# Two more ordinary block pairs, reuse of split weights at a half change, and two weight buffers instead of three

## The chip, the cores and the metric

The kernel runs on one core of one Trainium2 chip. The metric is the device time of the program in microseconds (us), the median of three runs; lower is better. TensorE (PE) multiplies matrices out of SBUF into PSUM, VectorE (DVE), ScalarE (ACT) and GpSimd (POOL) do the elementwise work, and SyncE (SP) holds the queue from which all transfers of this kernel are issued.

## The reference, cut to what matters

Three network blocks follow each other on one activation of 1024 tokens by 1024 features in float32. Two of them end in a feed-forward part, and these are what the change touches:

```python
# end of the first block: w_up is 1024 x 4096, w_down 4096 x 1024
up = jnp.square(jax.nn.relu(jnp.einsum('bsd,df->bsf', h2, w_up[l])))
x = x + jnp.einsum('bsf,fd->bsd', up, w_down[l])
...
# end of the third (last) block: w_up is 1024 x 5632, w_down 2816 x 1024
u = h @ w_up                                    # 5632 = 2 x 2816 columns
u = lax.conv_general_dilated(u, ...) + conv_b   # three taps along the tokens
gate, val = jnp.split(u, 2, axis=-1)
y = (jax.nn.gelu(gate, approximate=True) * val) @ w_down
x = x + rms_norm_3(y, ffn_post_norm[l])
```

## The kernel before, in words

Activations lie with features on the 128 partitions, in 8 blocks of features, and the 1024 tokens are cut into two halves of 512. Each float32 operand of a product is split in two parts, `hi` (a rounded copy, made on ACT) and `lo` (the rest, a subtraction on DVE or POOL); a product is then three matmuls, hi by hi, hi by lo and lo by hi (`mm3`, lines 179, 180, 181). `Env.split` (lines 143 and 145) makes the two parts.

`Env.chunk` loads one weight block (line 152, a 512 KB transfer on SP's queue for a full block) into a buffer `raw` and splits it into `whi` and `wlo`. Each of the three names has two buffers in the pool `wp`. Inside `e.third()` a further pool `wx` gives a third `whi` and `wlo`; `e.turn` counts the chunks, and every third one goes to `wx`.

**Ordinary units.** `Env.dense` multiplies one weight block with one half of the tokens: 8 blocks of features by three matmuls, 24 matmuls of 512 columns. In the last block, a feed-forward pair is a gate block `f` and its value block `22 + f`. The first `n0 = 4` pairs are done in ordinary units (line 1923): a loop over the two halves, in each over the four pairs, in each over the two blocks, so 16 units and 384 matmuls; the weight of each unit is loaded and split anew, so each block's weight twice. A unit is followed by the convolution (`conv`, lines 1897 to 1902, and `conv_rest`, lines 1907 and 1908), then by the GELU (line 1914) or the product and its store to DRAM (`put_up`, lines 1917 and 1918). In the first half, three steps of a generator (`join` for the second half of the tokens: residual, norm and split, lines 1454 to 1456, 250, 254, 263 and 143/145) are taken after each unit; what is left of it is run at the change of halves. In the second half each unit takes one step of `right_forms` (the sums and differences of activation blocks that the next part needs, lines 762 to 773), and the last two units one step of `left_forms` (the same for weights, lines 789 to 814).

**Strassen units.** The other 18 pairs go through `strassen`: each pair, both halves of the tokens, in seven products of four block steps, 84 matmuls instead of the 96 that a pair takes in ordinary units. Its weight forms use the buffers of `wp` as work space. In its last unit the loading of the down product's first activations (`FfnDown.load`, line 896 and a split) is interleaved.

**Down product.** `FfnDown.run` multiplies groups of up to six stored blocks by their weights: one chunk for each output block, which serves both halves (36 matmuls in a group of six), except in the last group, where the halves follow each other and each chunk serves one product of 15 matmuls. In the last block this runs inside `with e.third()`, opened after the pool `str` of the Strassen stage (its `c` tiles are what `put_up` stores from) is closed. While the second half of the last group is multiplied, the first half's residual and norm run (`end`).

The first block's feed-forward has the same stages with `n0 = 6` single blocks per half (line 690, 12 units), 13 Strassen units, and its down product runs with the two buffers of `wp` alone.

**What sets the order.** The program is written in the order above, but a planner at build time orders each engine's instructions by a simulated timeline (`schedule_with_timeline_sim=True`): an instruction whose inputs the simulation has ready can move ahead of ones written earlier that wait. On the chip each engine then runs its own list strictly in order, and SP its queue of transfers.

Of the kernel before, what the change touches and what calls it, by code (L numbers as in the profile page):

```python
# [46 lines left out]
class Ring:  # L47


    def __init__(self, views):  # L50
        self.views, self.i = views, 0

    def next(self):
        v = self.views[self.i % len(self.views)]
        self.i += 1
        return v
# [294 lines left out]
def block1(e, next_gain):  # L351


    nc, tc, io = e.nc, e.tc, e.io
# [4 lines left out]
    def load_x(h, ks=range(NK)):  # L359
        xs = []  # L360
        for k in ks:
            if k % 2 == 0:
                x = e.slot("x0")
            nc.sync.dma_start(x[:, k % 2], io["xT"][k][:, half(h)])
            xs.append(x[:, k % 2])
        return xs
# [3 lines left out]
    xs, hs, rc = [load_x(0, range(4))], [], []  # L370
# [292 lines left out]
    hs = [[], []]  # L663
    for f in range(0, NK, 4):
        ws = e.chunk(io["w1_out"][f : f + 4, :, 6:].rearrange("f p k o -> p f (k o)"), (4, 256), pool_lo=True)
        for j in range(4):
            w = [t[:, j].rearrange("p (k o) -> p k o", k=2) for t in ws]
# [12 lines left out]
    with ExitStack() as c2:  # L680
        tmp = c2.enter_context(tc.tile_pool(name="str", bufs=8))

        def act(f, h, src, dst):

            nc.scalar.activation(dst, src, AF.Relu)
            nc.scalar.activation(dst, dst, AF.Square)
            nc.sync.dma_start(upd[f, :, h], dst)

        n0 = 6
        fm, w = {}, {}  # L690
        weight = lambda u, i: io["w1_up"][n0 + 2 * u + i]
        forms, left = iter(()), iter(())
        units = [(f, h) for h in range(2) for f in range(n0)]
        wc = e.chunk(io["w1_up"][0])
        for i, (f, h) in enumerate(units):
            if i == n0:
                for _ in steps:
                    pass
                xs = [[a[:, j] for a in acc] for j in range(2)]
                acc.clear()  # L700
                forms, left = right_forms(e, xs, hs, fm), left_forms(e, weight, 0, w, tmp)
            p = e.dense(wc, hs[h])
            if i + 1 < len(units):
                wc = e.chunk(io["w1_up"][units[i + 1][0]])
            act(f, h, p, tmp.tile([P, HALF], F32, tag="c", name="c"))
            next(steps, None)
            next(forms, None)
            if h and f >= n0 - 2:
                next(left, None)
        hs = p = None  # L710
        for _ in left:
            next(forms, None)
        for _ in forms:
            pass

        def post(u, i, h, p):
            act(n0 + 2 * u + i, h, p, tmp.tile([P, HALF], F32, tag="c", name="c"))

        down = FfnDown(e, (6, 6, 5, 5, 5, 5), upd, io["w1_down"])
        strassen(e, tmp, fm, (32 - n0) // 2, weight, post, w, down.load(0))  # L720
        fm.clear()

# [22 lines left out]
def right_forms(e, xs, hs, fm):  # L745

    nc = e.nc
    fm.update(B11=hs[0][:4], B21=hs[0][4:], B22=hs[1][4:], T1=[], T2=[], T3=[], T4=[])

    def put(name, t):
        y = e.slot("act", dt=F32R)
        e.split(y[:, 0], y[:, 1], t)
        fm[name].append(y)

    for k in range(4):  # L760
        b11, b12, b22 = xs[0][k], xs[1][k], xs[1][k + 4]
        nc.vector.tensor_tensor(b11, b12, b11, op=ALU.subtract)
        nc.vector.tensor_tensor(b12, b22, b12, op=ALU.subtract)
        nc.vector.tensor_tensor(b22, b22, b11, op=ALU.subtract)
        put("T2", b22)
        put("T1", b11)
        yield
    for k in range(4):
        put("T3", xs[1][k])
        yield  # L770
    for k in range(4):
        b21, b22 = xs[0][k + 4], xs[1][k + 4]
        nc.vector.tensor_tensor(b21, b21, b22, op=ALU.subtract)
        put("T4", b21)
        yield
    for x in xs:
        x.clear()
# [44 lines left out]
def strassen(e, tmp, fm, n, weight, post, w, then):  # L822

    nc = e.nc  # L830

    def product(p, w, a, b, start, last):
        y, x = w.pop(a), fm.pop(b) if last else fm[b]
        for k in range(4):
            e.mm3(p, (y[:, 0, k], y[:, 1, k]), (x[k][:, 0], x[k][:, 1]), start and k == 0, k == 3, True)

    def first(w, last):
        ps = [e.pd() for _ in range(3)]
        product(ps[0], w, "A11", "B11", True, last)
        nc.scalar.activation(ps[1], ps[0], AF.Copy)  # L840
        return ps

    ps = first(w, n == 1)
    for u in range(n):
        last = u == n - 1
        nxt = {}
        pre = iter(()) if last else left_forms(e, weight, u + 1, nxt)

        def step():
            next(pre, None)  # L850
            if last:
                for _ in range(2):
                    next(then, None)

        product(ps[2], w, "S1", "T1", True, last)
        c22 = e.tsq()
        nc.scalar.activation(c22, ps[2], AF.Copy)
        step()
        product(ps[1], w, "S2", "T2", False, last)
        c12 = e.tnt()  # L860
        nc.scalar.activation(c12, ps[1], AF.Copy)
        step()
        product(ps[0], w, "A12", "B21", False, last)
        post(u, 0, 0, ps[0])
        step()
        product(ps[1], w, "S3", "T3", False, last)
        nc.vector.tensor_tensor(c22, ps[1], c22, op=ALU.add)  # L867
        step()
        follow = None if last else first(nxt, u + 2 == n)
        product(ps[1], w, "A22", "T4", False, last)  # L870
        post(u, 1, 0, ps[1])
        post(u, 1, 1, c22)
        step()
        product(ps[2], w, "S4", "B22", False, last)
        nc.vector.tensor_tensor(c12, ps[2], c12, op=ALU.add)
        post(u, 0, 1, c12)
        step()
        w, ps = nxt, follow
    for _ in then:
        pass  # L880


class FfnDown:
# [623 lines left out]
def block3(e, acc, hs, rest, out):  # L1507
    nc, tc, io = e.nc, e.tc, e.io
# [38 lines left out]
    with ExitStack() as c2:  # L1547
# [213 lines left out]
        units = [(i, h) for i in range(4) for h in range(2)]  # L1761
# [8 lines left out]
        order = (0, 4, 1, 5, 2, 6, 3, 7)  # L1770
# [17 lines left out]
    hs = [[], []]  # L1788
# [95 lines left out]
    hs = hn  # L1884
# [25 lines left out]
    def gelu(f, h, p, c):  # L1910
        conv(f, p, h, c)
        if h:
            conv_rest(f, c)
        nc.scalar.activation(c, c, AF.Gelu_apprx_tanh)
# [5 lines left out]
    with ExitStack() as c2:  # L1920
        tmp = c2.enter_context(tc.tile_pool(name="str", bufs=8))
        new = lambda: tmp.tile([P, HALF], F32, tag="c", name="c")
        n0 = 4
        fm, w = {}, {}
        weight = lambda u, i: io["w3_up"][n0 + u + 22 * i]
        forms, left = iter(()), iter(())
        units = [(b, h) for h in range(2) for f in range(n0) for b in (f, 22 + f)]
        wc = e.chunk(io["w3_up"][0])
        for i, (b, h) in enumerate(units):
            if i == 2 * n0:  # L1930
                for _ in steps:
                    pass
                forms, left = right_forms(e, xn, hs, fm), left_forms(e, weight, 0, w, tmp)
            p = e.dense(wc, hs[h])
            if i + 1 < len(units):
                wc = e.chunk(io["w3_up"][units[i + 1][0]])
            c = new()
            if b < 22:
                gelu(b, h, p, c)
                cg = c  # L1940
            else:
                conv(b, p, h, c)
                if h:
                    conv_rest(b, c)
                put_up(b - 22, h, cg, c)
            for _ in range(3):
                next(steps, None)
            next(forms, None)
            if h and i >= len(units) - 2:
                next(left, None)  # L1950
        hs = hn = p = c = cg = None
        for _ in left:
            next(forms, None)
        for _ in forms:
            pass

        cs = {}

        def post(u, i, h, p):

            f = n0 + u
            c = new()
            if i == 0:
                gelu(f, h, p, c)
            else:
                conv(22 + f, p, h, c)
                if h:
                    conv_rest(22 + f, c)
            cs[i, h] = c
            if i != h:  # L1970
                put_up(f, h, cs.pop((0, h)), cs.pop((1, h)))

        down = FfnDown(e, (6, 6, 5, 5), upd, io["w3_down"])
        strassen(e, tmp, fm, 22 - n0, weight, post, w, down.load(0))
        fm.clear()

# [12 lines left out]
        yield  # L1989
        yield from add_x(e, ms, xs, g_fpost, r, [o[:, half(h)] for o in out], True)  # L1990

    with e.third():
        for _ in down.run(add, end):
            pass


def prep3(a):
# [71 lines left out]
```

## Time and profile before

| | |
|---|---|
| runs | 3394.65, 3396.74, 3396.5 us; median 3396.5 us |
| the profiled execution | 3399.09 us, its span 3397.3 us |
| mean granted TensorE clock | 0.97 of full speed |
| PE busy | 3174.9 us, 93% of the span |
| DVE busy | 2119.8 us, 62% |
| ACT busy | 1504.1 us, 44% |
| POOL busy | 698.0 us, 21% |

The span is the time from the first to the last instruction of the one execution that was profiled. Busy shares are means over stages with different limits. The first block's ordinary units begin at about 599 us of the span, its down product runs from about 930 us; the last block's ordinary units begin at 2667.7 us, its Strassen units end at 3123.3 us and its down product follows to 3377.9 us.

### The profile page before, as it was taken

To read this page: it belongs to the slowest core of one execution; us is meant where nothing else is said; L and a number is where in the kernel's file an instruction comes from. 1 tells how busy PE (TensorE), PEld (TensorE's weight loads), DVE (VectorE), ACT (ScalarE), POOL (GpSimd) and SP (SyncE) were. 2 spreads that over 40 slices of the span, in tenths; PEclk is the share of its full clock that TensorE was granted. 3 is DMA by queue.
4 is the path that set the end of the run, shared out by engine and by line. 5 is a ranking of instruction groups with operands and counts; after the bars stand their busy time and mean duration, and the time that the engine had idled before them with its cause. 6 is when DMAs were issued, how large, how long until landed. Compare 5 with 4: busy or idle time off the path is not lost.

```text
span 3397.3 us, 43416 instructions
## 1 busy us (share of the span) xinstructions
PE 3174.9 (93%) x16044; PEld 2645.4 (78%) x16044; DVE 2119.8 (62%) x3795; ACT 1504.1 (44%) x2710; POOL 698.0 (21%) x451
## 2 busy tenths in 40 slices
PE   7999999999999998889999899989999989998997
PEld 6789877788888877667677777778887768886886
DVE  7666566654435366965776567666636687886336
ACT  4454453454532123433644565654434444454312
POOL 3000024000000004521444444435333200000001
PEclk9999999999999999899999899999999999998999
DMA  4112134433444234355644122225422432223333
GB/s 130 41 57 61 54 112 155 143 109 109 143 130 131 75 96 136 97 141 178 199 158 127 59 66 66 84 79 180 131 69 99 149 99 83 85 79 100 121 114 102
DMA packets 157572, 369.17 MB, mean 109 GB/s; under 512 B 20912, under 2 KB 29488, under 8 KB 157360
## 3 DMA queue, kind: packets, MB, share of 16 engines
q1 hardware_dynamic: 157360, 366.40, 33.8%
q8 instruction: 126, 2.06, 0.3%
q14 instruction: 86, 0.70, 0.1%
HBM read 286.64 MB, written 72.88 MB: 106 GB/s over the span
## 4 chain that ended last, share of the span: by engine, by line
PE 35%; DVE 9%; ACT 3%; issue 2%; DMA 1%; POOL 1%; SPq 0%; DVEq 0%; ACTq 0%; POOLq 0%
PE ps_d L179 10%; PE ps_d L180 10%; PE ps_d L181 10%; ACT whi L143 1%; DVE act L145 1%; DVE acc L1454 1%; POOL wlo L145 1%; PE ps_s L1737 1%; DVE hE L1723 0%; DVE wlo L145 0%; DVE hSA L1738 0%; DVE acc L1455 0%; DVE pr L1650 0%; DVE ssum L254 0%; PE ps_o L1320 0%
## 5 line engine op out<-in xcount | busy, mean ns | idle before, releaser
L143 ACT ACTIVATE whi<-raw 128x1024 fp32r<-128x1024 f32 (+2 forms) x328 | 317.3, 968 | 711.6 <-PE ps_d L180 601.9
L179 PE MATMUL ps_d<-act,whi 128*128 128x512 f32 x1280 | 512.8, 401 | 24.5 <-DVE acc L316 8.1
L181 PE MATMUL ps_d<-act,wlo 128*128 128x512 f32 x1280 | 508.4, 398 | 20.4 <-DVE wlo L145 19.5
L180 PE MATMUL ps_d<-act,whi 128*128 128x512 f32 x1280 | 508.9, 398 | 6.8 <-DVE act L145 6.7
L145 POOL TENSOR_TENSOR wlo<-raw,whi 128x1024 fp32r<-128x1024 f32 (+1 forms) x134 | 326.0, 2436 | 446.4 <-ACT whi L143 427.9
L179 PE MATMUL ps_d<-up,whi 128*128 128x512 f32 x864 | 337.5, 391 | 11.0 <-ACT whi L143 11.0
L179 PE MATMUL ps_d<-act,ws 128*128 128x512 f32 x868 | 335.0, 390 | 3.8 <-DVE sq L867 1.9
L180 PE MATMUL ps_d<-act,ws 128*128 128x512 f32 x868 | 338.4, 390 | 0.0
L180 PE MATMUL ps_d<-up,whi 128*128 128x512 f32 x864 | 337.2, 390 | 0.0
L181 PE MATMUL ps_d<-up,wlo 128*128 128x512 f32 x864 | 336.8, 390 | 0.0
L181 PE MATMUL ps_d<-act,ws 128*128 128x512 f32 x868 | 336.2, 390 | 0.0
L219 POOL TENSOR_TENSOR rr<-rv,mhalf 128x4 f32<-128x4 f32 (+1 forms) x43 | 45.6, 1060 | 1363.4 <-DVE rv L209 1177.2
L179 PEld LDWEIGHTS ps_d<-act,whi 128*128 128x128 f32 x1280 | 245.8, 192 | 80.8 <-ACT whi L143 14.6
L145 DVE TENSOR_TENSOR wlo<-raw,whi 128x1024 fp32r<-128x1024 f32 (+2 forms) x194 | 212.6, 1096 | 148.8 <-ACT whi L143 148.7
L181 PEld LDWEIGHTS ps_d<-act,wlo 128*128 128x128 f32 x1280 | 245.3, 192 | 73.9 <-DVE wlo L145 22.6
L180 PEld LDWEIGHTS ps_d<-act,whi 128*128 128x128 f32 x1280 | 245.7, 192 | 57.6 <-DVE act L145 7.5
L179 PE MATMUL ps_d<-mix,whi 128*128 128x512 f32 x512 | 201.0, 399 | 6.8 <-DVE acc L635 4.3
L181 PE MATMUL ps_d<-mix,wlo 128*128 128x512 f32 x512 | 201.6, 395 | 5.7 <-POOL wlo L145 5.7
L180 PE MATMUL ps_d<-mix,whi 128*128 128x512 f32 x512 | 203.1, 397 | 1.3 <-DVE mix L145 1.1
L179 PEld LDWEIGHTS ps_d<-up,whi 128*128 128x128 f32 x864 | 163.0, 189 | 45.6 <-ACT whi L143 11.7
L179 PEld LDWEIGHTS ps_d<-act,ws 128*128 128x128 f32 x868 | 163.2, 188 | 38.7 <-ACT ps_d L840 2.7
L181 PEld LDWEIGHTS ps_d<-act,ws 128*128 128x128 f32 x868 | 163.3, 188 | 34.1
(438 smaller groups left out, 6643.3 us busy)
## 6 DMA issues: line engine op xcount, KB each, us to landing
raw<-in_w_up SPq DMA_DIRECT2D x90, 512.0 KB, 3.9
raw<-in_w_fm SPq DMA_DIRECT2D x84, 512.0 KB, 3.8
upd<-c SPq DMA_DIRECT2D x108, 256.0 KB, 2.8
nq<-upd SPq DMA_DIRECT2D x108, 256.0 KB, 2.9
raw<-in_w_out SPq DMA_DIRECT2D x42, 512.0 KB, 3.8
xd<-acc SPq DMA_DIRECT2D x80, 256.0 KB, 2.4
raw<-in_w_down SPq DMA_DIRECT2D x64, 320.0 KB, 3.0
acc<-xd SPq DMA_DIRECT2D x64, 256.0 KB, 5.7
```

Of the source, the lines that this page charges most:

```text
L143: nc.scalar.activation(hi, src, AF.Copy)
L145: e.tensor_tensor(lo, src, hi.bitcast(F32), op=ALU.subtract)
L179: nc.tensor.matmul(out, lhsT=wh, rhs=xh, start=start, stop=False, skip_group_check=more)
L180: nc.tensor.matmul(out, lhsT=wh, rhs=xl, start=False, stop=False, skip_group_check=more)
L181: nc.tensor.matmul(out, lhsT=wl, rhs=xh, start=False, stop=stop, skip_group_check=more)
L219: self.nc.gpsimd.tensor_tensor(r, v, self.mhalf.broadcast_to([P, n]), op=ALU.pow)
L1454: nc.vector.scalar_tensor_tensor(m, m, g[:, k : k + 1], r, op0=ALU.mult, op1=ALU.mult)
L1737: nc.tensor.matmul(s[:, blk(j, 64)], lhsT=x[:, blk(j)], rhs=xv[:, nb * j : nb * j + nb, 1], start=True, stop=True)
```

## The change

There are four edits. In the last block the number of ordinary pairs goes from 4 to 6, so 24 ordinary units and 16 Strassen units; the steps of `join` taken after each unit go from three to two. In both blocks, the weights of the ordinary units go through a small class `Ahead`, which keeps the last two chunks: if the next unit's block is among them, nothing is loaded or split. The order of blocks in the second half is changed so that it begins with the two blocks that the first half ended with: blocks 4, 5, 0, 1, 2, 3 in the first block, pairs 5, 0, 1, 2, 3, 4 in the last. The condition for the steps of `left_forms` is reworded to mean the same last two units. In the last down product, `with e.third()` is dropped.

```diff
@@ first block @@
-        units = [(f, h) for h in range(2) for f in range(n0)]
-        wc = e.chunk(io["w1_up"][0])
+        units = [(f, 0) for f in range(n0)] + [(f - 2 if f > 1 else n0 - 2 + f, 1) for f in range(n0)]
+        ahead = Ahead(e, io["w1_up"], [f for f, h in units])
...
-            p = e.dense(wc, hs[h])
-            if i + 1 < len(units):
-                wc = e.chunk(io["w1_up"][units[i + 1][0]])
+            p = e.dense(ahead.get(i), hs[h])
+            ahead.get(i + 1)
...
-            if h and f >= n0 - 2:
+            if i >= len(units) - 2:
                 next(left, None)
@@ new @@
+class Ahead:
+    def __init__(self, e, src, order):
+        self.e, self.src, self.order, self.have = e, src, order, []
+
+    def get(self, i):
+        if i >= len(self.order):
+            return None
+        f = self.order[i]
+        for g, w in self.have:
+            if g == f:
+                return w
+        w = self.e.chunk(self.src[f])
+        self.have = self.have[-1:] + [(f, w)]
+        return w
@@ last block @@
-        n0 = 4
+        n0 = 6
...
-        units = [(b, h) for h in range(2) for f in range(n0) for b in (f, 22 + f)]
-        wc = e.chunk(io["w3_up"][0])
+        units = [(b, h) for h in range(2) for f in range(n0) for b in ((f - h) % n0, 22 + (f - h) % n0)]
+        ahead = Ahead(e, io["w3_up"], [b for b, h in units])
...
-            for _ in range(3):
+            for _ in range(2):
                 next(steps, None)
...
-    with e.third():
-        for _ in down.run(add, end):
-            pass
+    for _ in down.run(add, end):
+        pass
```

## Rows read from the trace of the kernel before

**Rows 1.** Busy time by stretch, last block: engines, PEclk, DMA share, GB/s
```profile
2667.50:2776.30 108.80, 94.66 (x406) 76.56 (x407) 90.08 (x148) 49.03 (x72) 7.61 (x6) 0.95 0.36 119
2782.04:3116.80 334.76, 334.76 (x1476) 276.94 (x1476) 270.84 (x510) 170.98 (x284) 0.00 (x0) 1.00 0.27 85
3123.30:3134.48 11.18, 0.14 (x1) 0.00 (x0) 7.29 (x16) 4.23 (x7) 0.00 (x0) 0.65 0.34 117
3134.48:3140.20 5.72, 5.72 (x14) 4.45 (x15) 0.94 (x1) 0.00 (x0) 0.00 (x0) 0.50 0.25 69
3140.20:3377.90 237.70, 237.70 (x1052) 196.33 (x1050) 99.73 (x142) 64.29 (x100) 6.86 (x5) 1.00 0.36 112
```

**Rows 2.** What PE waited for, 2667 to 2790 us: total, times, longest
```profile
PE ps_d L180 <- DVE act L145: 6.7, 1, 6.7
PE ps_d L181 <- DVE wlo L145: 3.9, 1, 3.9
PE ps_d L179 <- ACT whi L143: 1.8, 2, 1.2
PE ps_d L179 <- ACT act L143: 1.7, 1, 1.7
```

**Rows 3.** PE's timeline behind the two long waits: start, duration
```profile
2724.92 0.63 PE L179 MATMUL ps_d<-act,whi 128*128 128x512 f32 x1
...
2742.01 0.63 PE L179 MATMUL ps_d<-act,whi 128*128 128x512 f32 x1
```

**Rows 4.** DVE's groups, 2667.5 to 2776 us: busy, mean ns
```profile
L145 DVE TENSOR_TENSOR wlo<-raw,whi 128x1024 fp32r<-128x1024 f32 x15 | 18.3, 1220 | 11.1 <-ACT whi L143 11.1
L145 DVE TENSOR_TENSOR act<-acc,act 128x512 fp32r<-128x512 f32 x20 | 12.7, 685 | 0.0
L1898 DVE SCALAR_TENSOR_TENSOR c<-ps_d,g_ffn_conv,c 128x511 f32<-128x511 f32 x15 | 11.1, 743 | 0.0
...
L1455 DVE TENSOR_TENSOR acc<-acc 128x512 f32<-128x512 f32 x4 | 3.8, 958 | 0.0
```

**Rows 5.** DVE's and ACT's timelines at the change of halves, last block
```profile
2714.89 5.36 DVE L263 SCALAR_TENSOR_TENSOR acc<-acc,g_ffn_pre_norm,ps_t 128x512 f32<-128x512 f32 x8 [1.87 <-PE ps_t L228]
2733.63 2.20 ACT L143 ACTIVATE act<-acc 128x512 fp32r<-128x512 f32 x4 [12.72 <-DVE acc L764]
2740.14 1.22 DVE L145 TENSOR_TENSOR wlo<-raw,whi 128x1024 fp32r<-128x1024 f32 x1
```

**Rows 6.** What waited for what, 3116 to 3141 us
```profile
PE ps_d L179 <- ACT whi L143: 11.0, 1, 11.0
...
ACT whi L143 <- DMA upd<-c: 2.8, 1, 2.8
...
PE ps_d L179 <- DVE sq L867: 1.9, 1, 1.9
```

**Rows 7.** Timelines of SP, DVE and ACT around the last down product's start
```profile
3075.31 0.33 SPq L152 DMA_DIRECT2D raw<-in_w_down  x1
...
3102.89 0.95 DVE L145 TENSOR_TENSOR wlo<-raw,whi 128x768 fp32r<-128x768 f32 x1
...
3127.83 0.68 DVE L145 TENSOR_TENSOR up<-nq,up 128x512 fp32r<-128x512 f32 x1
...
3129.15 2.69 SPq L1918 DMA_DIRECT2D upd<-c  x2
3133.59 0.84 ACT L143 ACTIVATE whi<-raw 128x768 fp32r<-128x768 f32 x1 [2.83 <-DMA upd<-c]
```

**Rows 8.** First block's ordinary units, 600 to 700 us: PE's longest wait, DVE's timeline
```profile
PE ps_d L181 <- DVE wlo L145: 3.2, 1, 3.2
...
625.14 1.21 DVE L145 TENSOR_TENSOR wlo<-raw,whi 128x1024 fp32r<-128x1024 f32 x1
```

**Rows 9.** Busy time over the first block's down product, columns as in rows 1
```profile
930.00:1268.00 338.00, 338.00 (x1501) 280.05 (x1500) 155.44 (x230) 86.60 (x132) 3.42 (x4) 1.00 0.34 108
```

**Rows 10.** DVE's timeline in the last group of the last down product
```profile
3365.08 5.35 DVE L1454 SCALAR_TENSOR_TENSOR acc<-acc,g_ffn_post_norm,ps_t 128x512 f32<-128x512 f32 x8
```

More of the change, by code (lines that the diff above doesn't have):

```diff
@@ L1933, in block3 @@
                 forms, left = right_forms(e, xn, hs, fm), left_forms(e, weight, 0, w, tmp)
-            p = e.dense(wc, hs[h])
-            if i + 1 < len(units):
-                wc = e.chunk(io["w3_up"][units[i + 1][0]])
+            p = e.dense(ahead.get(i), hs[h])
+            ahead.get(i + 1)
             c = new()
@@ L1945, in block3 @@
                 put_up(b - 22, h, cg, c)
-            for _ in range(3):
+            for _ in range(2):
                 next(steps, None)
             next(forms, None)
-            if h and i >= len(units) - 2:
+            if i >= len(units) - 2:
                 next(left, None)
```

## The prediction

> **What bounds the kernel now.** I read the busy times by stretch over the last block first [rows 1]: where PE is busy for the whole stretch, only fewer matmuls help; where it is not, a wait can go. The Strassen stretch and nearly the whole down product are full. A matmul of 512 columns starts every 0.227 us (334.76 us by 1476) at full clock. Two stretches are not full: the ordinary units (94.66 of 108.80 us busy) and the start of the down product, where PE stands still for 11.2 us and then runs 14 matmuls at granted clock 0.50. The list of PE's waits [rows 2, 6, 8] names what ended each gap, the timelines [rows 3, 5, 7, 10] show why, and the groups of DVE [rows 4] give the prices.
>
> In the ordinary units PE lost 6.7 + 1.7 us at the change of halves, waiting for the second half's normalised activations, and 3.9 us plus a part of 1.8 us two units later, waiting for a weight's split [rows 2]. DVE was the late one: at the change it still ran eight normalisations (5.36 us), and ACT sat 12.72 us in front of a split of an activation form that waited for DVE, with the next weight's split queued behind it; that weight's `wlo` came at 2740.14 [rows 5]. After both long waits PE ran low: 13 matmuls (7 and 6) of 0.63 us like those shown [rows 3], at half the full clock, the level of 1.2 GHz.
>
> At the down product PE waited 11.0 us for a `whi`, and that one waited for a store `upd<-c` [rows 6]. Its weight had been loaded since 3075.31, and another chunk was complete at 3102.89 + 0.95 us [rows 7]. The first chunk fell to the pool `wx`, which lies where the closed pool `str` was, so its split had to wait for the last store out of a `c` tile.
>
> **Two more ordinary pairs.** 2 x (96 - 84) = 24 more matmuls, 24 x 0.227 = **+5.4 us** on PE, which is the path here. Their convolutions, GELUs and stores exist either way; they move out of Strassen units into ordinary ones.
>
> **The ordinary stage's waits.** First half before: 8 units of 24 matmuls are 43.5 us of PE. DVE has per unit a `wlo` (1.22), two convolution steps (0.743 each, the second taken as the first), half a product (0.34) and a short copy (taken at 0.15), 3.2 us [rows 4]; and from `join` 8 x 4 operations of 0.685 to 0.743 plus four additions of 0.958 that POOL does not take, about 28 us with its reductions. 25.6 + 28 = 54 against 43.5: DVE is 10 us late, and the two waits at the change are 8.4. After: 12 units, 65.3 us of PE against 38.4 + 28 = 66 of DVE: even. Two steps per unit are still 24 steps in the half, and `join` takes 19. Second half before: 8 x 3.5 (two short ones of `conv_rest`, taken at 0.2 each, for the copy) + 32 form operations of 0.685 and 11 weight form operations of the same size = 57 against 43.5. After: 12 x 3.5 - 2 x 1.22 for the two reused blocks + 29 = 69 against 65.3. These sums use whole durations, which overlap by some 0.08 us each, so DVE fits with a little to spare. At the change, the first two units need no new `whi` or `wlo`, so the 10.9 us of these two units cover the forms that now stand ahead of a split.
>
> To be had in this stage: 6.7 + 1.7 + 3.9 + 1.8 = 14.1 us of waits and 3.6 us of low clock (13 x 0.2 and two slow first matmuls of some 0.5 more). I take **-13 us**: the two waits at the change go (8.4) with their low clock (2), and of the rest 2.6 of 7.3 goes, since one late split behind forms may stay. Next late is DVE again, by a few us at most. Bounds: 0, all 14.1 + 3.6 = 17.7.
>
> **The reuse of split weights** removes per block two loads on SP's queue, two ACT splits and two `wlo`; in the last block that is counted above. Nothing on SP or POOL is moved past other work. In the first block the one long wait (3.2 us for a `wlo` done at 625.14 + 1.21 [rows 8]) is in the fifth unit, in the first half, behind normalisations and forms that the planner put ahead; the reused blocks are the seventh and eighth units. So **0**. Bounds: the wait goes through another order, with 0.9 us of small ones and ten matmuls at low clock, -6; a new wait of the same size, +3.
>
> **Two weight buffers in the last down product.** The first chunk then goes to `wp`, whose buffers are free when the last weight forms are made; the chunk ready at 3103.8 shows it. The activations do not hold PE: the last of the first group's twelve was split by 3128.5 [rows 7], while PE, from 3123.4, needs it in the second product's last block, 33 matmuls or 7.5 us later. So the 11.0 us go, and of the 14 matmuls at low clock, (5.72 / 14 - 0.227) x 14 = 2.5 us, about 1, because the 1.9 us wait [rows 6] that comes before stays and lowers the clock for a while: **-12.5 us**; at least -3 if the last store's own chain were still on the path, at most -13.6.
>
> For the rest of it, one buffer fewer means that a `whi` can be made only when the product before last has ended. In the last group that leaves 15 x 0.227 = 3.4 us for an ACT split and a `wlo`, some 1.6 us, and for what DVE has queued. The nearest row is the first block's down product, the same sizes with two buffers: 338.00 of 338.00 us busy [rows 9], so the price is **0**. The upper end is the burst of eight steps of `add_x` (5.35 us [rows 10]) in front of one `wlo`: 5.35 + 1.6 - 3.4 = +3.6, and +5 with low clock; below 0 there is nothing, as this stretch is full [rows 1].
>
> The Trainium skill (Perfetto Trace Analysis, Identifying Performance Opportunities) says that a gap which repeats on the engine that should be saturated can mean too few buffers; that speaks against dropping the third. The first block's row does not agree for these sizes; by the rule this term would be that of the second rival.
>
> **Sum.** 5.4 - 13 + 0 - 12.5 + 0 = -20.1 us. The profiled execution took 3399.1, so 3379.0; the median of the runs lies 2.6 below that execution: **3376.5 us**. A measurement of this kernel can tell about 0.2%, 6.8 us, from no change: below 3389.7 is faster, above 3403.3 slower.
>
> **Rivals.** (1) *DVE stays late in the ordinary stage.* The sums above are near a tie, and the planner's order, not the sum, made the wait two units after the change. Against it: two units without splits stand there. If all 17.7 us come back at other units: 5.4 - 12.5, 3389.4 us. (2) *Two buffers starve the last group*, the slower side. Place: each of its 16 chunks, where the split must follow the product two before. It decides once the queue ahead of a `wlo` on DVE is longer than 3.4 - 1.6 = 1.8 us. If it is longer by 1.7 us at each of the 16 chunks, 27 us are lost and the time is 3403.7. For it: the burst [rows 10] is such a queue; against it: the first block shows no such wait in 338 us. (3) *The first block's wait goes too*, because the build-time order changes with the program: 3376.5 - 6 = 3370.5. For it: such orders are fragile; against it: all that stands before the fifth unit is unchanged. (4) *The down product's first chunk is held by something else*, for instance the last convolutions on DVE, which end only just before the last store: then the third edit gives 3 us and the time is 3386. Against it: ACT's wait names the store [rows 6], and the other chunk was split 30 us earlier.
>
> **How the numbers follow.** Forecast 0.60, rival 1 0.18, rival 2 0.05, rival 3 0.10, rival 4 0.07. The forecast, rivals 3 and 4 and about half of rival 1 lie below 3389.7: 0.84 faster; the other half and a little of rival 2 within 0.2%: 0.12; slower 0.04. The range takes in the forecast with its bounds (some 8 us either way), rival 3 and rival 1: 3366 to 3391; it leaves out rival 2 and the tails.
>
> **What would show it.** Right: no PE wait of over 2 us at the change of halves of the last block, 576 ordinary and 1344 Strassen matmuls there; the first down matmul within 1 us of the last Strassen one, and no `whi` waiting for a store; the down product full until the last chunk; the first block's 3.2 us unchanged. Wrong: `act` or `wlo` from DVE among PE's long waits in the last block's ordinary units, a repeated wait for `whi` or `wlo` in the last group, or the same 11 us gap ended by another instruction.

## The result and the profile after

The changed kernel takes 3371.42 us (median; 3367.7 to 3373.64), beside 3395.57 us (3392.57 to 3396.74) of the kernel before on the same chip: a ratio of 0.9931, 95% interval 0.9918 to 0.9943, or -24.2 us (-19 to -28). Forecast were 3376.5 us, 3366 to 3391, and -20.1. So it is faster, inside the range, by some 4 us more than the sum said.

The profiled execution after took 3367.7 us, its span 3365.6 (before: 3399.1 and 3397.3), mean granted clock 0.975 (0.970). Between the two spans lie 31.7 us. They split by stage like this: the first block from its first ordinary matmul to its first down matmul 4.7 (316.8 to 312.1; that down matmul starts at 915.4 us of the span in before, not at about 930 as said above), the untouched stretch behind it 4.6, the last block from its first ordinary matmul to its last down matmul (the last one of line 179) 22.3 (709.5 to 687.2). The 4.6 are no effect: that stretch, counted from the end of the first block's down product, took 1397.6 us in the profiled execution of before, and 1389.3 to 1396.1 in the thirteen others of this study, none of which changes it. It scatters by some 7 us, and before's is the longest; the medians, 24.2 apart, are the better measure of the whole.

Busy time by stretch of the kernel after (columns: us, PE busy, PEld, DVE, ACT, POOL, PEclk, DMA share, GB/s): first block's ordinary and Strassen units, last block's ordinary units, start, body and end of its down product.

```profile
598.34:910.40 312.06, 309.57 (x1364) 255.11 (x1365) 159.98 (x233) 163.51 (x295) 7.00 (x5) 1.00 0.38 119
2658.08:2792.70 134.62, 130.31 (x570) 106.43 (x571) 109.00 (x180) 61.42 (x88) 7.62 (x6) 0.99 0.37 121
3094.60:3107.00 12.40, 12.40 (x56) 10.26 (x56) 10.99 (x23) 5.53 (x9) 0.00 (x0) 1.00 0.37 124
3107.00:3330.00 223.00, 223.00 (x990) 184.66 (x989) 93.22 (x137) 65.48 (x101) 1.38 (x1) 1.00 0.37 115
3330.00:3345.90 15.90, 13.42 (x57) 10.03 (x55) 15.03 (x22) 3.56 (x6) 6.00 (x4) 1.00 0.43 153
```

Against [rows 1] the ordinary stage has turned from 94.66 busy of 108.80 to 130.31 of 134.62, and the start of the down product is full, where 11.2 us were empty and 5.72 ran at 0.50. New is a loss of 2.5 us in the last row. What PE waited for in the kernel after, first 2640 to 2830 us, then 3060 to 3366 us (total, times, longest):

```profile
PE ps_d L179 <- ACT whi L143: 2.3, 3, 1.2
PE ps_d L181 <- DVE wlo L145: 2.0, 1, 2.0
...
PE ps_d L181 <- DVE wlo L145: 2.2, 1, 2.2
...
PE ps_d L179 <- ACT whi L143: 0.3, 1, 0.3
```

The 6.7 and 1.7 us for `act` at the change of halves [rows 2] are gone; one `wlo` wait of 2.0 us is left. The 11.0 us for `whi` and the 1.9 us for `sq` (a sum of the last Strassen unit, made on DVE) [rows 6] are gone too. (Lines behind the new class are some 18 higher than before.)

PE's timeline in the kernel after at the change from Strassen to down product, ACT's split of the first down weight, and SP's last store of the stage:

```profile
3099.63 0.39 PE L179 MATMUL ps_d<-up,whi 128*128 128x512 f32 x1
...
3105.30 0.39 PE L179 MATMUL ps_d<-act,ws 128*128 128x512 f32 x1
...
3107.79 0.39 PE L181 MATMUL ps_d<-act,ws 128*128 128x512 f32 x1
```
```profile
3060.74 0.85 ACT L143 ACTIVATE whi<-raw 128x768 fp32r<-128x768 f32 x1 [0.59 <-DMA raw<-in_w_down]
```
```profile
3104.93 0.32 SPq L1936 DMA_DIRECT2D upd<-c  x1
```

The first down weight is split 44 us before the last store; before, it waited for that store [rows 7]. And the down product does not follow the Strassen units, it fills them: from 3099.63 to 3105.30 PE runs 25 down matmuls (5.67 us at 0.227) ahead of the last twelve Strassen ones, where it stood for 1.9 us before.

In the first block, at the wait of [rows 8], PE's timeline of the kernel before, then PE's and DVE's of the kernel after:

```profile
622.51 0.50 PE L179 MATMUL ps_d<-act,whi 128*128 128x512 f32 x1 [0.47 <-ACT whi L143]
622.85 0.39 PE L180 MATMUL ps_d<-act,whi 128*128 128x512 f32 x1
626.41 0.79 PE L181 MATMUL ps_d<-act,wlo 128*128 128x512 f32 x1 [3.16 <-DVE wlo L145]
627.00 0.63 PE L179 MATMUL ps_d<-act,whi 128*128 128x512 f32 x1
```
```profile
622.24 0.50 PE L179 MATMUL ps_d<-act,whi 128*128 128x512 f32 x1 [0.47 <-ACT whi L143]
...
623.78 0.40 PE L180 MATMUL ps_d<-act,whi 128*128 128x512 f32 x1
626.15 0.50 PE L181 MATMUL ps_d<-act,wlo 128*128 128x512 f32 x1 [1.98 <-DVE wlo L145]
626.49 0.39 PE L179 MATMUL ps_d<-act,whi 128*128 128x512 f32 x1
```
```profile
624.88 1.21 DVE L145 TENSOR_TENSOR wlo<-raw,whi 128x1024 fp32r<-128x1024 f32 x1
```

DVE's split is as late as before (624.88 in a span that runs 0.3 us ahead; 625.14 in [rows 8]). But PE now runs six matmuls that need only `whi` before it waits, where it had two. The wait is 1.98 us in place of 3.16, and the matmuls behind it take 0.39 us; before, ten of 0.63 us stood there.

### The profile page after: what moved, and what is told of

Its sections match the earlier page's. It is cut to its first block, busy times and chain, and to the rows that moved or that the text cites. A ratio compares the mean times of both kernels' runs of the same rounds, so it can differ in the third digit from the quotient of the medians.

```text
span 3365.6 us, 43389 instructions
## 1 busy us (share of the span) xinstructions
PE 3168.2 (94%) x16068; PEld 2639.7 (78%) x16068; DVE 2104.8 (63%) x3773; ACT 1497.0 (44%) x2694; POOL 695.8 (21%) x451
## 4 chain that ended last, share of the span: by engine, by line
PE 37%; DVE 7%; ACT 3%; issue 2%; DMA 1%; POOL 1%; SPq 0%; DVEq 0%; ACTq 0%; POOLq 0%
PE ps_d L179 11%; PE ps_d L181 11%; PE ps_d L180 11%; ACT whi L143 1%; DVE acc L1472 1%; POOL wlo L145 1%; DVE act L145 1%; PE ps_s L1755 0%; DVE hSA L1756 0%; DVE hE L1741 0%; DVE acc L1473 0%; PE ps_o L1338 0%; DVE wlo L145 0%; DVE hx L1746 0%; PE ps_d L1766 0%
## 5 line engine op out<-in xcount | busy, mean ns | idle before, releaser
L179 PE MATMUL ps_d<-act,whi 128*128 128x512 f32 x1344 | 535.6, 398 | 21.0 <-DVE acc L316 8.1
L181 PE MATMUL ps_d<-act,wlo 128*128 128x512 f32 x1344 | 531.4, 397 | 15.8 <-DVE wlo L145 14.7
L180 PE MATMUL ps_d<-act,whi 128*128 128x512 f32 x1344 | 532.1, 396 | 0.1
L179 PEld LDWEIGHTS ps_d<-act,whi 128*128 128x128 f32 x1344 | 256.7, 191 | 78.5 <-ACT whi L143 13.8
L180 PE MATMUL ps_d<-act,ws 128*128 128x512 f32 x812 | 315.9, 389 | 0.0
L181 PE MATMUL ps_d<-act,ws 128*128 128x512 f32 x812 | 313.9, 389 | 0.0
L181 PEld LDWEIGHTS ps_d<-act,wlo 128*128 128x128 f32 x1344 | 256.0, 190 | 72.6 <-DVE wlo L145 19.5
L179 PE MATMUL ps_d<-act,ws 128*128 128x512 f32 x812 | 312.3, 389 | 0.0
L180 PEld LDWEIGHTS ps_d<-act,whi 128*128 128x128 f32 x1344 | 256.4, 191 | 53.0 <-issue 1.1
L181 PEld LDWEIGHTS ps_d<-up,wlo 128*128 128x128 f32 x864 | 162.2, 188 | 36.5 <-DVE wlo L145 3.0
L179 PEld LDWEIGHTS ps_d<-up,whi 128*128 128x128 f32 x864 | 162.2, 188 | 34.4 <-ACT whi L143 0.7
L180 PEld LDWEIGHTS ps_d<-up,whi 128*128 128x128 f32 x864 | 162.2, 188 | 33.5
```

The source lines that it names most:

```text
L179: nc.tensor.matmul(out, lhsT=wh, rhs=xh, start=start, stop=False, skip_group_check=more)
L180: nc.tensor.matmul(out, lhsT=wh, rhs=xl, start=False, stop=False, skip_group_check=more)
L181: nc.tensor.matmul(out, lhsT=wl, rhs=xh, start=False, stop=stop, skip_group_check=more)
```

## How the experiments are read

All ratios are to the kernel before, timed beside it on the same chip; its medians there were 3394.2, 3396.1 and 3397.1 us in the three sets. Since effects of 5 us are at the edge of what times tell, each kernel is also read by stage, from its one profiled execution. *First block* is the time from the first ordinary to the first down matmul. *Lost, ordinary* is 165 us from the first ordinary matmul of the last block, less 0.2268 us (334.76 / 1476, [rows 1]) for each matmul in them. *Lost, rest* is what is lost from there to the start of the last down matmul of the first kind (hi by hi), against 2952 matmuls with four pairs, 2964 with five, 2976 with six. Sixteen short transposes count as matmuls in the first of these columns and so are missing in the second: that column is some 4 us too high in every kernel, and 4.0 in it means that next to nothing is lost.

| kernel | ratio, 95% interval | first block | matmuls in 165 us | lost, ordinary | lost, rest |
|---|---|---|---|---|---|
| before | 1 | 316.8 | 647 | 18.3 | 21.7 |
| after | 0.9931 (0.9918 to 0.9943) | 312.1 | 704 | 5.3 | 6.9 |
| no third buffer | 0.9958 (0.9946 to 0.9971) | 316.2 | 639 | 20.1 | 8.3 |
| third buffer, other turn | 0.9968 (0.9955 to 0.9981) | 316.6 | 641 | 19.6 | 10.6 |
| pairs | 1.0008 (1.0 to 1.0017) | 315.5 | 670 | 13.0 | 22.9 |
| reuse | 1.0002 (0.9993 to 1.0011) | 312.0 | 633 | 21.4 | 21.9 |
| reuse, first block only | 0.9995 (0.9987 to 1.0004) | 312.1 | 642 | 19.4 | 21.0 |
| pairs, reuse | 0.9973 (0.9963 to 0.9983) | 312.2 | 704 | 5.3 | 22.9 |
| pairs, no third | 0.9951 (0.9938 to 0.9963) | 316.2 | 676 | 11.7 | 8.3 |
| reuse, no third | 0.9957 (0.9945 to 0.997) | 313.6 | 631 | 21.9 | 8.6 |
| pairs, no third, late forms | 0.9957 (0.9945 to 0.997) | 315.7 | 672 | 12.6 | 6.9 |
| after, late forms | 0.993 (0.9918 to 0.9942) | 312.5 | 701 | 6.0 | 8.6 |
| after, five pairs | 0.9928 (0.9916 to 0.994) | 312.0 | 690 | 8.5 | 7.0 |
| after, third buffers late | 0.9918 (0.9905 to 0.993) | 312.6 | 704 | 5.3 | 4.0 |

Four kernels with the same ordinary stage (before, the two with the buffer alone, reuse in the first block only) read 18.3 to 20.1, so a column is good to about 1 us. What six pairs cost in matmuls, 5.4 us, is in none of the lost columns and is to be added.

## The experiments

**The third buffer alone.** The theory: the first down chunk falls to the pool that lies where `str` was, and waits for its last store. Rival 4: something else holds it. Two ways to send that chunk elsewhere:

```diff
-    with e.third():
-        for _ in down.run(add, end):
-            pass
+    for _ in down.run(add, end):
+        pass
```


> The kernel before with one edit alone: the last down product without the third weight buffer. Theory (the first chunk's buffer lay where the store's tiles were): the 11 us wait at the start of the last down product and the matmuls at the lower clock behind it go, about -13 us against the kernel before; a late split of 2 to 3 us may come near the end of the last group, as in the changed kernel, so -10 to -14. Rival (something else holds that chunk): -3 us at most, with the gap ended by another instruction. The ordinary units of both blocks stay as they were (waits of 6.7, 3.9 and 3.2 us).

```diff
     with e.third():
+        e.turn = 2
         for _ in down.run(add, end):
             pass
```


> The kernel before with the third buffer kept, but the count of chunks set so that the first two chunks of the last down product go to the two ordinary buffers and only the third one to the extra buffer. Theory (which chunk fell to the extra buffer made the wait, not the number of buffers): the same -10 to -14 us as dropping the third buffer, and without a late split at the end, so up to 2.5 us better than that. Rival (a third buffer as such costs): no gain, the 11 us wait stays.

Without the buffer 3379.66 us (-14.6), with it and another turn 3382.86 (-11.4). PE's waits from 3060 to 3385 us in the first, then the second:

```profile
...
PE ps_d L181 <- DVE wlo L145: 2.2, 1, 2.2
...
PE ps_d L179 <- ACT whi L143: 0.3, 1, 0.3
```
```profile
PE ps_d L179 <- DMA nq<-upd: 3.9, 1, 3.9
...
```
and in the second, from 3126 to 3136 us, PE's weight load (PEld), the store and ACT:
```profile
PEld ps_d L179 <- ACT whi L143: 4.4, 1, 4.4
...
3129.80 0.32 SPq L1918 DMA_DIRECT2D upd<-c  x1
...
3133.05 1.58 ACT L143 ACTIVATE whi<-raw 128x768 fp32r<-128x768 f32 x2 [1.12 <-DMA raw<-in_w_down]
```

What is left out are the two waits of the final norm, which stand in every kernel. The gap is gone in both, so it was the place of the first chunk and not the number of buffers: with three buffers and another turn it goes as well. The second kernel has a wait of 3.9 us, up to 3134.68, that the first has not. The list of waits names the load of an activation for it, but the weight load of the same matmul waited for a `whi`, and that one ended at 3134.63. It is the second of the two in ACT's row; in the trace it waits for that last store, which landed at 3133.72. So the third chunk, now the one in `wx`, was held as the first had been, for less time and two chunks later. It is the same cause once more. The first has instead the 2.2 and 0.3 us in the last group, which the second, with its third buffer, has not: the price of two buffers.

**Pairs alone, reuse alone.** The kernel before with six pairs and two steps of `join` per unit; and the changed kernel with four pairs, three steps and the third buffer, so that only the reuse is left, in both blocks.

```diff
-        n0 = 4
+        n0 = 6
...
-            for _ in range(3):
+            for _ in range(2):
```


> The kernel before with six ordinary pairs and two steps per unit in the last block alone; weights are loaded twice as before and the third buffer stays. Theory (VectorE was late in the first half, and the longer half gives it time): the waits of 6.7 and 1.7 us at the change of halves go, +5.4 us of matmuls come, and a late weight split at the change may stay since nothing is reused, so -2 to -9 us. Rival (the reuse at the change is what removes the waits): they stay, and the time is 3 to 6 us longer than before.

> The kernel before with the reuse of split weights and the new order of blocks in both blocks alone; four pairs in the last block, third buffer kept. Theory (the first block's gain comes from the planner, which now puts six more hi matmuls of the unit ahead of the late split): the first block's ordinary stage is 3 to 5 us shorter, its wait 2.0 us in place of 3.2; in the last block the 6.7 us at the change stays and the 3.9 us of the late split goes or moves: -3 to -10 us in all. Rival (the reuse changes nothing, the first block's gain in the profile was chance): 0 within 3 us, and the first block's 3.2 us unchanged.

The pairs measured 1.0008, the reuse 1.0002: neither gains anything by itself. In the last block the lost time falls by 5 to 7 us with the pairs, which is what they cost. With the reuse it does not fall (21.4): PE's wait of 3.9 us for a `wlo` shrinks to 0.7, but the `act` wait stays (5.7), the waits for `whi` grow from 1.8 to 3.9, and a wait for a `ps_d` that ACT copies at the start of the Strassen units grows from 1.3 to 3.2. "Pairs" means the sixth pair and the fewer steps of `join` per unit together, "reuse" the kept weights and the new order of blocks together; no run takes these apart. In the pairs' trace the `act` wait at the change is gone and a `wlo` wait has come, in PE's and DVE's timelines:

```profile
2746.29 0.50 PE L179 MATMUL ps_d<-act,whi 128*128 128x512 f32 x1 [0.47 <-ACT whi L143]
2752.83 0.79 PE L181 MATMUL ps_d<-act,wlo 128*128 128x512 f32 x1 [5.81 <-DVE wlo L145]
```
```profile
2744.21 6.70 DVE L145 TENSOR_TENSOR act<-acc,act 128x512 fp32r<-128x512 f32 x11
...
2751.56 1.22 DVE L145 TENSOR_TENSOR wlo<-raw,whi 128x1024 fp32r<-128x1024 f32 x1
```

Eleven `lo` parts of activation forms stand on DVE in one row, 6.70 us, ahead of the weight's `wlo`, whose `whi` ACT had begun at 2743.58.

**Pairs and reuse together, without the third edit.** The changed kernel with `with e.third()` put back.

> The changed kernel with the third weight buffer of the last down product put back: two more pairs and the reuse, without the third edit. Alone, the pairs measured +4 us (1.0008) and the reuse +0.7 us (1.0002), of which the first block's profile shows -4.3. Theory A (pairs and reuse help only together: each alone moves the wait of the ordinary stage to another place): about -10 to -13 us against before, ratio near 0.9965; PE's waits in the last block's ordinary units sum to under 5 us, and the 11 us gap at the down product is still there. Theory B (the ordinary stage was never worth more than its price of 5.4 us, and the rest of the gain comes from the third edit once the weights are reused): between -2 and +3 us, ratio 0.9995 to 1.001.

The ratio is 0.9973 (-9.0 us), and only 5.3 us are lost in the ordinary stage, as in the changed kernel. Its waits from 3060 us on show the gap in its old size, and in its ordinary stage (2650 to 2840 us) what is left:

```profile
PE ps_d L179 <- ACT whi L143: 11.0, 1, 11.0
...
PE ps_d L179 <- ACT whi L143: 2.3, 3, 1.2
PE ps_d L181 <- DVE wlo L145: 2.0, 1, 2.0
```

So theory A holds: pairs and reuse help together. In the last block alone, from its first ordinary to its last down matmul, before takes 709.5 us, pairs 710.9, reuse 712.8, and both 703.2, where the sum of the single effects would be 714.2. The first block's profile adds 4.6 to these 6.3 us, 10.9 where the medians show 9.0. Why it is so, the kernel after shows beside the pairs' rows above (PE's, then DVE's timeline):

```profile
2745.25 0.50 PE L179 MATMUL ps_d<-act,whi 128*128 128x512 f32 x1 [0.47 <-ACT whi L143]
2748.01 0.79 PE L181 MATMUL ps_d<-act,wlo 128*128 128x512 f32 x1 [2.03 <-DVE wlo L145]
```
```profile
2739.26 5.51 DVE L145 TENSOR_TENSOR act<-acc,act 128x512 fp32r<-128x512 f32 x9
...
2746.72 1.23 DVE L145 TENSOR_TENSOR wlo<-raw,whi 128x1024 fp32r<-128x1024 f32 x1
```

The burst is there with nine in a row. Counted from the first ordinary matmul (2658.08 after, 2661.85 with the pairs alone), the late `wlo` starts at 88.6 us in place of 89.7. But PE comes to it after 380 matmuls (16 transposes among them), at 87.9 us, in place of 356 at 85.2. That is one unit of 24 later: the late weight is now that of the second half's fourth unit and not of its third, since the first two units make none. 1.1 us earlier and 2.7 later are the 3.8 us between the waits of 5.81 and 2.03. The rest of the difference (13.0 to 5.3) is small waits around the change (0.92, 0.54 and 0.28 us in the pairs' trace, not there in the other) and low clock.

**Reuse in the first block alone.** The last block as before.

> Before, with the reuse of split weights in the first block alone; the last block is as before. Theory A (the first block's gain is the planner's new order ahead of the late split, and belongs to the reuse there): -3 to -5 us, ratio 0.9985 to 0.9991, the long PE wait in the first block 2 us where it was 3.2, with the clock at 1.00 around it. Theory B (the difference between the two profiles' first blocks is scatter): 0, ratio within 0.9995 to 1.0005.

By the times it is inconclusive: -3.0 us between medians, but the interval of the ratio (0.9987 to 1.0004) holds both theories. By stage it is not: the first block takes 312.0 to 313.6 us in all eight kernels with the reuse there, and 315.5 to 316.8 in all six without, 3.8 us between the means. Its wait there is 2.0 us, with the clock at 1.00, as in the changed kernel.

**Two of the three edits, the other ways.** Pairs without reuse or third buffer; and reuse with four pairs and no third buffer.

> Before, with six ordinary pairs (two steps of join per unit) and without the third weight buffer, but every weight loaded and split again. If the edits simply add, +4 and -14 give -10 us, ratio near 0.997. Theory A (pairs need the reuse at the change of halves): -8 to -12 us, with a wlo wait of some 5 us at the change of halves as in the run of the pairs alone. Theory B (the removal of the buffer is worth more once the pairs are there): -16 us or more, ratio under 0.9955.

> The changed kernel with four ordinary pairs and three steps of join per unit: the reuse in both blocks and no third buffer. If the edits simply add, +0.7 and -14 give -13 us, ratio near 0.996. Theory A (reuse needs the two more pairs, which give DVE the time to be on time at the change): -12 to -15 us, and act from DVE still among PE's long waits there, 5 to 7 us. Theory B (the reuse and the buffer's removal are what interact): -20 us or more, ratio under 0.994.

They measured 0.9951 and 0.9957. Every kernel without the buffer (and without later buffers) has 6.9 to 8.6 us lost in the rest, every one with it in its old place 21.0 to 22.9: the third edit is worth about 14 us whatever else is done. The 6.9 to 8.6 fall in two groups by the clock behind the `wlo` wait of the last group: in the kernels with 6.9 or 7.0 PE goes on at full clock there, in those with 8.3 or 8.6 it drops to matmuls of 0.63 us. The pairs without reuse have their 5.8 us `wlo` again (11.7 lost), the reuse with four pairs its `act` wait of 5.7 (21.9 lost). The first of the two came out at -16.6 us by its ratio, against an additive -10; its columns against before's give +5.4 - 6.6 - 13.4 = -14.6, the plain sum of the parts by stage. By stage the pairs' own +2.7 us was off, inside its interval (0 to +5.8), so theory B is not needed, though its ratio came out.

**Forms taken two units later.** If the burst of form parts ahead of the split is the cause, writing the forms behind it should do what the reuse does.

```diff
-            next(forms, None)
+            if i >= 2 * n0 + 2:
+                next(forms, None)
```


> Six ordinary pairs and no third buffer, every weight loaded anew (this measured 0.9951), with one thing moved: the first two units of the second half take no step of the activation forms, so that no form stands ahead of the weight splits at the change of halves. The trace without this has one wlo wait of 5.8 us there; that wlo stood on DVE behind eleven act parts in a row (6.70 us). Theory A (order: the reuse helps since the forms stood ahead of a split, and any edit that lets the splits go first does the same): the 5.8 us wait falls under 1 us, and the time falls by 5 to 8 us more, to a ratio near 0.993, without any reuse. Theory B (load: DVE has too much to do at the change, and the reuse takes two splits of 1.22 us and their queue away): the wait stays above 3 us or moves to a unit right behind; ratio 0.9945 or more.

> The changed kernel with the same move of the forms by two units. Theory A: the last wlo wait of 2.0 us of the changed kernel's ordinary stage and the six matmuls at low clock behind it go: -3 to -4 us, ratio to before near 0.992. Theory B: no change, or a new wait at the start of the Strassen stage from the forms that are then late: 0 to +4 us, ratio 0.993 to 0.9945.

They measured 0.9957 and 0.993: nothing is gained, and the `wlo` waits are 5.6 and 2.0 us, nearly as without the edit (5.8 and 2.0). But that does not speak for theory B, since ahead of the late `wlo` the edit changed nothing on the chip. DVE's timeline of the first of the two has the same eleven in a row there:

```profile
2745.85 6.70 DVE L145 TENSOR_TENSOR act<-acc,act 128x512 fp32r<-128x512 f32 x11
...
2753.20 1.21 DVE L145 TENSOR_TENSOR wlo<-raw,whi 128x1024 fp32r<-128x1024 f32 x1
```

The planner took these forms forward again, though they were written later; only behind the late `wlo` did two of them move. Whether another order on DVE would make the reuse needless stays open.

**Five pairs.** The prediction's sums have DVE near a tie with six.

```diff
-        n0 = 6
+        n0 = 5
```


> The changed kernel with five ordinary pairs in the last block in place of six: PE does 12 matmuls fewer, 2.7 us. Theory A (DVE and PE are near a tie with six pairs: each pair gives DVE some 3.8 us per half): DVE is about 5 us late in the first half, so act from DVE comes back among PE's waits at the change with 2 to 4 us, and the time is 0 to +4 us against the changed kernel, ratio to before 0.993 to 0.9945. Theory B (the reuse at the change had made the sixth pair needless): -2.7 us, ratio 0.9923.

It measured 0.9928 beside 0.9931, no difference that these times could tell. It loses 3.2 us more in the ordinary stage (8.5 to 5.3) and has 2.7 us less to multiply. PE's waits from 2640 to 2840 us:

```profile
PE ps_d L179 <- ACT whi L143: 3.0, 4, 1.1
...
PE ps_d L181 <- DVE wlo L145: 1.3, 1, 1.3
...
PE ps_d L180 <- DVE act L145: 0.4, 2, 0.2
```

`act` is back among the waits, with 0.2 us at a time and not the 2 to 4 expected. By these columns the sixth pair buys about what it costs.

**Third buffers where they are needed.** The changed kernel loses 2.5 us in the last group. Its DVE, ACT and PE timelines there:

```profile
3329.38 2.71 DVE L1472 SCALAR_TENSOR_TENSOR acc<-acc,g_ffn_post_norm,ps_t 128x512 f32<-128x512 f32 x4
3332.01 0.98 DVE L145 TENSOR_TENSOR wlo<-raw,whi 128x640 fp32r<-128x640 f32 x1
...
3339.09 0.81 DVE L145 TENSOR_TENSOR wlo<-raw,whi 128x640 fp32r<-128x640 f32 x1
```
```profile
3336.26 0.74 ACT L143 ACTIVATE whi<-raw 128x640 fp32r<-128x640 f32 x1 [3.04 <-DMA raw<-in_w_down]
```
```profile
3337.05 0.50 PE L179 MATMUL ps_d<-up,whi 128*128 128x512 f32 x1 [0.31 <-ACT whi L143]
3339.96 0.50 PE L181 MATMUL ps_d<-up,wlo 128*128 128x512 f32 x1 [2.18 <-DVE wlo L145]
```

Four steps of `add_x` push the `wlo` at 3332.01 back; that `wlo` holds a `raw` buffer, so the last load starts late, `whi` waits for it, and the last `wlo` falls behind more of `add_x`. The edit gives the last group a third `raw`, `whi` and `wlo`, from a pool opened only there:

```diff
+            if last and third:
+                e.raw3 = True
+                stack.enter_context(e.third())
...
+        raw = (wp if self.raw3 else self.wp).tile(shape, F32, tag="raw", name="raw")
```


> The changed kernel with a third buffer for raw, whi and wlo in the last group of the last down product alone, opened long after the last store of the Strassen stage. Theory A (two buffers cost the last group its wlo wait of 2.2 us and the whi wait of 0.3 us, because the chunk behind DVE's burst can't be made ahead): both go, -2.5 us, ratio to before near 0.9923. Theory B (the burst holds DVE's queue whatever the buffers): the waits stay, ratio 0.993.

This kernel takes 3367.32 us, a ratio of 0.9918. The down product is then full from its start to the last matmul (busy time by stretch, columns as above), with the burst of eight as in [rows 10] but behind the split:

```profile
3098.00:3346.00 248.00, 248.00 (x1098) 204.91 (x1097) 117.67 (x179) 73.83 (x114) 6.84 (x5) 1.00 0.38 119
```
```profile
3332.58 0.81 DVE L146 TENSOR_TENSOR wlo<-raw,whi 128x640 fp32r<-128x640 f32 x1
3333.31 5.35 DVE L1479 SCALAR_TENSOR_TENSOR acc<-acc,g_ffn_post_norm,ps_t 128x512 f32<-128x512 f32 x8
```

Theory A holds: lost in the rest are 4.0 us in place of 6.9, and both waits are gone. By the stage this kernel beats the changed kernel; by the times it is faster than before, and its interval overlaps with that of the changed kernel.

## Why the prediction was right, and where it was off

*Two more pairs, +5.4, and the ordinary stage's waits, -13.* Right, as a pair of terms: lost time fell from 18.3 to 5.3, 13.0 us, and the kernel with pairs and reuse alone shows the same 5.3. The two waits at the change went with their low clock (8.4 + 2), one late split behind forms stayed, 2.0 us. DVE was the late engine, as said, and the near tie is real: with five pairs `act` is back, if only with 0.4 us in all. That the total agrees to the tenth is luck. Of the late split only some 1 us went, not 2.6, and some 1.4 came from a wait that the sum left out, in PE's list for 2667 to 2790 us:

```profile
PE ps_d L179 <- ACT ps_d L840: 1.3, 1, 1.3
```

It stands at the start of the Strassen units and is not there in the kernel after; why it went was not traced. The low clock to be had was also a little less than the 3.6 us of the sum: of the 13 slow matmuls 11 took 0.63 us and two 0.5. What the text hardly weighed is that the reuse carries the term: it stood in one sentence ("the first two units need no new `whi` or `wlo`"), and without it the pairs pay only their own way. Rival 1 (all lost time comes back at other units) is what the reuse does without the pairs.

*Reuse in the first block, 0.* This step failed: "all that stands before the fifth unit is unchanged" holds for the program as written, and for DVE's order ahead of the late split, and not for PE's. The planner took four more matmuls ahead of it. It is rival 3, inside its bound of -6: -4.7 us in the two profiles, -3.8 between the means of all kernels with and without. From the first ordinary to the first down matmul, before (columns as above):

```profile
598.64:915.40 316.76, 312.04 (x1365) 256.83 (x1366) 162.32 (x235) 165.51 (x298) 6.99 (x5) 0.99 0.38 121
```

PE's busy time fell from 312.04 to 309.57 us for the same work, and its idle time from 4.72 to 2.49: of the 4.7, 2.5 are low clock and 2.2 waits. Why the planner's timeline came out otherwise was not traced.

*The start of the down product, -12.5.* The cause was right (the chunk's place in a pool over a closed one; rival 4 fell) and the size too small. The 11.0 us went, but also the 1.9 us for `sq` that the text let stay, and with it the low clock that it kept: with a down weight ready 40 us early, the planner put down matmuls into that wait. Lost time in the rest fell from 21.7 to 4.0 where nothing else is in the way (third buffers late), 17.7 us against 12.5: 12.9 of waits and, by difference, 4.8 of low clock.

*Two buffers in the rest, 0.* Mis-sized: 2.9 us (6.9 against 4.0 with late third buffers), 2.5 of them idle, inside the bounds 0 to +3.6, and by the mechanism that set the upper one, the burst of `add_x` ahead of a `wlo`. Where the clock drops behind the wait it is 4.3 to 4.6, inside the +5 that the text gave with low clock. The first block's row was the wrong neighbour, since it has no such burst. Rival 2's place was right and its price not: one chunk of 16 was late. The Trainium skill (Perfetto Trace Analysis, Identifying Performance Opportunities) reads repeated gaps as a possible lack of buffers; here one gap of 2.2 us was that, and the one of 11.0 us came from a buffer more.

*The signs.* The text's own signs came out in part. The waits for `act` and the 11 us gap are gone, but the first block's 3.2 us changed, one `wlo` wait of 2.0 us is left among the ordinary units, and one of 2.2 us came in the last group, once and not at every chunk.

*Sum.* By stage of the profiles: -4.7, then +5.4 - 13.0, then -14.8 (-17.7 and +2.9), together -27.1; with the first block at its mean of -3.8, -26.2; timed were -24.2, interval -19 to -28. The forecast's -20.1 lacks the first block's 4 and is 2 short in the down product (-14.8 against -12.5), where two misses of 5 and 3 us went against each other.

## What to carry to other kernels

A pool opened where another was just closed inherits the last reader of what lay there: give the first use after a change of stages to buffers that are long free, and open extra ones where their place is free and a burst needs them. Edits that each take away one cause of the same lateness can measure zero apart (1.0008 and 1.0002) and 9 us together (0.9973), so undo them in pairs before calling one useless. When a planner orders the engines, neither "written earlier" nor "written later" fixes an order: compare each engine's list of the two traces, the engine that waits among them.

## What the runs showed of the hardware that was not expected

A wait of about 2 us on PE came out on either side of the clock's two levels. In the kernel after, the wait of 1.98 us in the first block left the matmuls behind it at 0.39 us, with the granted clock 1.00 over 618 to 632 us (2.4 GHz), and the wait of 2.03 us in the last block was followed by six of 0.63 us, the level of 1.2 GHz. Ahead of each stood a wait of 0.47 us; between the two waits PE ran six matmuls in the first case and two in the second. In the kernel with late third buffers, where it also ran two, the 2.00 us wait was followed by three matmuls of 0.50 to 0.40 us, one of 0.57, and only then by those of 0.63. The last group of the down product shows it with the same order on PE. In the kernel that only drops the third buffer, PE's timeline there is:

```profile
3347.64 0.50 PE L179 MATMUL ps_d<-up,whi 128*128 128x512 f32 x1 [0.27 <-ACT whi L143]
...
3350.59 0.79 PE L181 MATMUL ps_d<-up,wlo 128*128 128x512 f32 x1 [2.22 <-DVE wlo L145]
3351.18 0.63 PE L179 MATMUL ps_d<-up,whi 128*128 128x512 f32 x1
```

In the kernel after, whose rows at 3337.05 and 3339.96 us are shown above, the waits are 0.31 and 2.18 us, also with two matmuls between them, and the matmuls behind take 0.39 to 0.40 us. So a wait of this length costs its 2 us or, by six times 0.2, some 1.2 us more (1.4 between the columns of these two kernels), and which of the two is not to be read from its length, nor from PE's order around it.
